# Half of the output projection's first part is queued on TensorE behind the state-space stage's last product

## The chip, the cores and the metric

The kernel runs on one core of one Trainium2 chip. The metric is the device time of one execution in microseconds (us); the time before is the median of three runs. The profile is one further execution of the same program. The engines are named as in its views: PE is TensorE's matmuls and PEld its weight loads, DVE is VectorE, ACT is ScalarE, POOL is GpSimd, SP is SyncE, which issues most DMAs.

## The reference, cut to what matters

A backbone of two layers over 512 latent tokens and 256 context tokens, 1024 channels wide. In each layer one input projection feeds three parallel branches; their outputs are joined to 2048 channels and go through one output projection.

```python
for l in range(2):
    u = rmsnorm(h, norm_w[l]) * (1 + scale) + shift          # scale, shift, gate: from mod_w[l]
    parts = split(u @ w_in[l])
    ssd = ssd_branch(...)    # 1024 channels: chunked scan over 6 chunks of 128 tokens, both directions;
                             # y * silu(z), then an RMS norm over each of two halves (g = 0, 1)
    gla = gla_branch(...)    # 512 channels
    s5  = s5_branch(...)     # 512 channels, ends in a gated product with s5_glu_w
    h = h + gate * (concat(ssd, gla, s5) @ w_out[l])         # w_out[l]: 2048 x 1024
return rmsnorm(h_lat, final_norm_w)
```

In the second layer only the latent tokens are needed at the end.

## The kernel before, in words

The kernel is written against a framework that takes the instructions in program order, each with a rank by that order, and plans the order of every engine's queue by a simulation of its own; on the chip each queue is then worked off in that order. Nothing in the source fixes the order around the change: what is ready in the planner's simulation and ranks highest goes first, and an instruction of lower rank fills an engine that would be free.

Activations lie with channels on the partitions: 128 channels by 768 tokens, of which 256 are context. Every large product is made of three passes in a split float format (`PASSES`): weights and activations are each split into a high and a low half, `wsplit` (L408 the load `wr`, ACT the copy `wh`, DVE at L411 the difference `wl`) and `split` (ACT, DVE L416). The tiles `wr`, `wh`, `wl` and the accumulators `pl` have two buffers each, the residual tiles `cv` three, the tiles `cs` three, and the operand tiles `hl` eight.

The end of a layer, in program order:

- The state-space stage (`ssd_parts`): six steps i, each for two head groups g. `decay` builds a 128x1024 matrix with eight ACT and eight DVE pieces each (L903 to L917), `within` multiplies it into the chunk (L934), `between` adds what comes from the neighbouring chunk (L923, L925, L929) and updates the running state (L946 to L957). POOL issues the loads that these steps need.
- The gate blocks of z and the gated product of the s5 branch (L1046, L1048, DVE L1057, L1059) and the splitting of the two other branches' outputs into eight `hl` tiles.
- `ssd_norm(g)`: loads z (L968, into `cs`), multiplies, squares, sums over the partitions with a product on PE (L975), takes the root on ACT, scales (L983) and splits into the tiles bA and bB.
- `spilled_part`, the first part of the output projection: for each of eight output tiles m, `out_part` makes 24 products into `pl` (L1082, 512 latent tokens) and in layer 0 another 24 into `pc` (L1084, 256 context tokens), from the eight `hl` tiles. DVE adds gate times product to the old residual (L1095 and L1096 in layer 0, L1091 in layer 1), and the sum is stored to `hpD` (L1104).
- In layer 0 only: `mod_cols(1, ...)` twice, for scale and shift of layer 1: eight loads of 512 KB each into `hl` tiles (L1112) and 64 small products (L203) for each. They need `hl` buffers that the first part has let go.
- The second part: `out_part(m, 0, yss, ...)` for m = 0 to 7 over the normed state-space output, again L1082 and L1084, with the sum from `hpD` added (L1121 is its load). In layer 0 the same again for the gate of layer 1 follows (`mod_tiles(1, 16, 8)`, L230 and L203), then layer 1.

Of the kernel before, what the change touches and what calls it, by code (L numbers as in the profile page):

```python
# [2 lines left out]

# [37 lines left out]
def hybrid_backbone_kernel(  # L41
# [16 lines left out]
    V, S, G, PE = nc.vector, nc.scalar, nc.gpsimd, nc.tensor  # L58
# [10 lines left out]
    def T(tag, shape, bufs, dt=F32):  # L69
        uid[0] += 1  # L70
        return sb.tile(shape, dt, tag=tag, bufs=bufs, name=f"{tag}_{uid[0]}")
# [26 lines left out]
    def ps(n=512, p=128):  # L98
        uid[0] += 1
        return psp.tile([128, 512], F32, tag="ps", bufs=3, name=f"ps_{uid[0]}")[:p, :n]  # L100

    def pa(n=512, p=128):
        uid[0] += 1
        return psp.tile([128, 512], F32, tag="pa", bufs=2, name=f"pa_{uid[0]}")[:p, :n]
# [15 lines left out]
    def act(out, in_, f, **kw):  # L120
        return S.activation(out, in_, f, **kw)  # L121
# [344 lines left out]
    def layer(l, u):  # L466
# [5 lines left out]
        def proj(blocks, m=128, ctx_too=True, src=None, early=False):  # L472

            w = wsplit(src if src is not None else wblk[l, blocks], 8 * m)
            p_l, p_c = pl(), pc() if ctx_too else None
            seq = [(k, wi, ui) for k in range(8) for wi, ui in PASSES]
            if early:
                seq.sort(key=lambda a: a[2])
            for n, (k, wi, ui) in enumerate(seq):
                st, sp = n == 0, n == 23  # L480
                lhs = w[wi][:, k * m : (k + 1) * m]
                PE.matmul(p_l[:m], lhs, u[k][:, ui, LC:NT], start=st, stop=sp)  # L482
                if ctx_too:
                    PE.matmul(p_c[:m], lhs, u[k][:, ui, 0:LC], start=st, stop=sp)  # L484
            return p_c, p_l
# [19 lines left out]
        p_c, p_l = proj(None, m=64, src=wdl[l], early=last)  # L505
# [70 lines left out]
        for i in range(4):  # L576
            p_c, p_l = proj(BU + i, early=last and i == 0)
# [91 lines left out]
        for b4 in range(8):  # L669
            py = pa(4 * ncx)  # L670
# [209 lines left out]
        def ssd_parts(g, i):  # L880

            wk = wgs[g]
            cf, cbk = STEPS[i]
            c = cf
            xtok, bT, cT = xts[g], bcs[g][:, 0, :], bcs[g][:, 1, :]
            rf, rbw, ex, q2 = (wk[:, 1024 * j : 1024 * j + 1024].rearrange("p (h t) -> p h t", h=8) for j in range(4))
            hs = [wk[:, 4096 + 512 * d : 4608 + 512 * d] for d in range(2)]
            xw, bt = wk[:, 5632:6144], bts[g]
            y_at = lambda c: xy[:, 4 * g : 4 * g + 4, 128 * c : 128 * c + 128]

            reads = [i > 0 and not (last and cc < 2) for cc in (cf, cbk)]
            inner = not (last and c < 2)

            def load():

                gdma(wk[:, 0:2048].rearrange("p (d x) -> p d x", d=2),
                     bass.AP(tensor=acsD[l].tensor, offset=acsD[l][c, 0, 8 * g].offset,
                             ap=[[0, 128], [2048, 2], [1, 1024]]))

            def decay():  # L900
                pcb = pa(384)
                cb, cbl, cbu = (pcb[:, 128 * j : 128 * j + 128] for j in range(3))
                PE.matmul(cb, bT[:, 128 * c : 128 * c + 128], cT[:, 128 * c : 128 * c + 128], start=True, stop=True)  # L903
                V.tensor_tensor(cbl, cb, LE, MUL)
                V.tensor_tensor(cbu, cb, GE, MUL)
                for h in range(8):
                    ih = 16 * c + 8 * g + h
                    jd = 32 * c + 8 * g + h
                    act(q2[:, h, :], cbl, AF.Copy, scale=dtt[:, jd : jd + 1])
                    V.scalar_tensor_tensor(q2[:, h, :], cbu, dtt[:, jd + 16 : jd + 17], q2[:, h, :], MUL, ADD)  # L910
                for h in range(8):
                    ih = 16 * c + 8 * g + h
                    act(ex[:, h, :], rf[:, h, :], AF.Identity, bias=naf[:, ih : ih + 1])
                    V.scalar_tensor_tensor(ex[:, h, :], rbw[:, h, :], rb[:, ih : ih + 1], ex[:, h, :], SUB, MIN)
                exf, q2f = ex.rearrange("p h t -> p (h t)"), q2.rearrange("p h t -> p (h t)")
                act(exf, exf, AF.Exp)
                V.tensor_tensor(exf, exf, q2f, MUL)  # L917

            def incoming(d, cc, ep):

                po = ps()
                for t in range(4):
                    PE.matmul(po[:, 128 * t : 128 * t + 128], hs[d][:, 128 * t : 128 * t + 128],  # L923
                              cT[:, 128 * cc : 128 * cc + 128], start=True, stop=True)
                V.tensor_tensor(po, po, ep, MUL)  # L925
                return po

            def add(cc, p):
                V.tensor_tensor(y_at(cc), y_at(cc), p.rearrange("p (t x) -> p t x", t=4), ADD)  # L929

            def within():
                py = ps()
                for h in range(8):
                    PE.matmul(py[64 * (h % 2) : 64 * (h % 2) + 64, 128 * (h // 2) : 128 * (h // 2) + 128],  # L934
                              xtok(c)[:, 64 * h : 64 * h + 64], ex[:, h // 2 + 4 * (h % 2), :], start=True, stop=True)
                add(c, py)

            def between():
                for d, cc in ((0, cf), (1, cbk)):
                    if reads[d]:  # L940
                        add(cc, incoming(d, cc, eps[eput[0] % 3]))
                        ep_load(eput[0] + 3)
                        eput[0] += 1
                    if i < 5:
                        wv = wf[:, d, 16 * cc + 8 * g : 16 * cc + 8 * g + 8]
                        V.tensor_tensor(heads(xw), heads(xtok(cc)), per_head(wv), MUL)  # L946
                        pt = pa(128)
                        PE.transpose(pt, bT[:, 128 * cc : 128 * cc + 128], ident)
                        act(bt, pt, AF.Copy)
                        pst = ps()  # L950
                        PE.matmul(pst, bt, xw, start=True, stop=True)  # L951
                        if i == 0:
                            act(hs[d], pst, AF.Copy)
                        else:
                            jd = 32 * cc + 16 * d + 8 * g
                            V.tensor_tensor(heads(hs[d]), heads(hs[d]), per_head(dec[:, jd : jd + 8]), MUL)
                            V.tensor_tensor(hs[d], hs[d], pst, ADD)  # L957

            none = lambda: None
            return (decay, within, between, load) if inner else (none, none, between, none)  # L960
# [32 lines left out]
        wgs = [big("bA"), big("bB")]  # L993
        bts = [T("bt", [128, 128], 2) for _ in range(2)]

        eps = [wgs[0][:, 5120:5632], wgs[1][:, 5120:5632], T("s5p", [128, 576], 1)[:, 0:512]]
        eput = [0]
        euse = [(g, d, cc) for i in range(1, 6) for g in range(2) for d, cc in enumerate(STEPS[i]) if not (last and cc < 2)]

        def ep_load(n):  # L1000
            if n < len(euse):
                g, d, cc = euse[n]
                gdma(eps[n % 3], bass.AP(tensor=expD[l].tensor, offset=expD[l][cc, d, 8 * g].offset,
                                         ap=[[512, 2], [0, 64], [1, 512]]))
# [32 lines left out]
        for m in range(4):  # L1037
            wv = wsplit(wglu[l, m])
            pair = []
            for half in range(2):  # L1040
                p_l, p_c = pl(), None if last else pc()
# [31 lines left out]
        def out_part(m, k0, rhs, order):  # L1073
            nk = len(rhs)
            w = wsplit(wout[l, m, k0 // 8, :, 128 * (k0 % 8) : 128 * (k0 % 8) + 128 * nk], 128 * nk)
            p_l, p_c = pl(), None if last else pc()
            n = 0
            for kk in order:
                for wi, ui in PASSES:
                    lhs = w[wi][:, kk * 128 : kk * 128 + 128]  # L1080
                    st, sp = n == 0, n == 3 * nk - 1
                    PE.matmul(p_l, lhs, rhs[kk][:, ui, LC - t0 : NT - t0], start=st, stop=sp)  # L1082
                    if not last:
                        PE.matmul(p_c, lhs, rhs[kk][:, ui, 0:LC], start=st, stop=sp)  # L1084
                    n += 1
            return p_c, p_l
# [10 lines left out]

        def spilled_part(src, k0, rhs, order):
            for m in range(8):
                p_c, p_l = out_part(m, k0, rhs, order)  # L1100
                ho = cv(NT)
                dma(ho[:, t0:NT], src[128 * m : 128 * m + 128])
                residual(ho, ho, m, p_c, p_l)
                dma(hpD[l][128 * m : 128 * m + 128, t0:NT], ho[:, t0:NT])  # L1104
# [13 lines left out]
        for m in range(8):  # L1118
            p_c, p_l = out_part(m, 0, yss, range(len(yss)))
# [155 lines left out]
```

## Time and profile before

| | us |
|---|---|
| median of 3 runs | 1627.29 (1621.0 to 1630.99) |
| the profiled execution | 1629.74 |
| its span, first to last instruction | 1628.0 |
| PE busy | 1385.0 |
| DVE busy | 1216.1 |
| ACT busy | 651.1 |

The profiled execution is 1.7 us longer than its span and 2.4 us above the median of the runs. The mean granted clock of TensorE was 0.911 of its full 2.4 GHz.

### The profile page before, as it was taken

To read this page: it belongs to the slowest core of one execution; us is meant where nothing else is said; L and a number is where in the kernel's file an instruction comes from. 1 tells how busy PE (TensorE), PEld (TensorE's weight loads), DVE (VectorE), ACT (ScalarE), POOL (GpSimd) and SP (SyncE) were. 2 spreads that over 40 slices of the span, in tenths; PEclk is the share of its full clock that TensorE was granted. 3 is DMA by queue.
4 is the path that set the end of the run, shared out by engine and by line. 5 is a ranking of instruction groups with operands and counts; after the bars stand their busy time and mean duration, and the time that the engine had idled before them with its cause. 6 is when DMAs were issued, how large, how long until landed. Compare 5 with 4: busy or idle time off the path is not lost.

```text
span 1628.0 us, 23300 instructions
## 1 busy us (share of the span) xinstructions
PE 1385.0 (85%) x8536; PEld 1123.9 (69%) x8536; DVE 1216.1 (75%) x2487; ACT 651.1 (40%) x1159; POOL 110.4 (7%) x248
## 2 busy tenths in 40 slices
PE   3879885899499889998994898998989999979766
PEld 2657774778496766776872585887779887756545
DVE  8767757999478894499896636369966897798964
ACT  4212224222623622565442524334363446554452
POOL 0000001310000000001010000041000000010100
PEclk8889978999589989999997899999989999999978
DMA  8566567332155535446668432642336443446522
GB/s 324 139 140 194 155 162 191 101 117 82 34 167 162 188 99 157 129 153 179 219 214 274 154 123 90 181 152 91 121 114 186 124 142 124 137 136 198 169 71 97
DMA packets 154658, 243.85 MB, mean 150 GB/s; under 512 B 48688, under 2 KB 89648, under 8 KB 154544
## 3 DMA queue, kind: packets, MB, share of 16 engines
q1 hardware_dynamic: 130096, 211.82, 42.8%
q0 software_dynamic: 24448, 30.54, 6.6%
q8 instruction: 67, 1.10, 0.3%
q14 instruction: 47, 0.39, 0.1%
HBM read 192.81 MB, written 49.38 MB: 149 GB/s over the span
## 4 chain that ended last, share of the span: by engine, by line
PE 45%; DVE 25%; DMA 16%; ACT 7%; issue 6%; SPq 1%; DVEq 0%; ACTq 0%; POOLq 0%
PE pl L482 13%; PE pl L1082 9%; PE pc L484 4%; DMA gD<-cs 4%; DMA bc<-lpD 3%; PE pc L1084 3%; ACT bA L121 2%; DMA cs<-zD 2%; DVE wl L411 2%; PE ps L951 2%; PE pl L1046 1%; PE pl L704 1%; PE ps L923 1%; PE pa L392 1%; ACT bB L121 1%
## 5 line engine op out<-in xcount | busy, mean ns | idle before, releaser
L482 PE MATMUL pl<-hl,wh 128*128 128x512 f32 (+1 forms) x1184 | 405.4, 410 | 18.8 <-DVE ev L501 14.5
L482 PEld LDWEIGHTS pl<-hl,wh 128*128 128x128 f32 (+1 forms) x1184 | 223.8, 193 | 75.0 <-DVE ev L501 15.1
L482 PE MATMUL pl<-hl,wl 128*128 128x512 f32 (+1 forms) x592 | 241.6, 409 | 18.1 <-DVE wl L411 18.1
L121 ACT ACTIVATE wh<-wr 128x1024 fp32r<-128x1024 f32 (+1 forms) x122 | 127.9, 1051 | 286.4 <-PE pc L484 95.7
L411 DVE TENSOR_TENSOR wl<-wr,wh 128x1024 fp32r<-128x1024 f32 (+1 forms) x122 | 147.8, 1213 | 66.1 <-ACT wh L121 52.8
L484 PE MATMUL pc<-hl,wh 128*128 128x256 f32 (+1 forms) x864 | 189.9, 293 | 5.8 <-ACT hl L121 4.7
L484 PEld LDWEIGHTS pc<-hl,wh 128*128 128x128 f32 (+1 forms) x864 | 145.2, 193 | 16.4 <-issue 5.7
L482 PEld LDWEIGHTS pl<-hl,wl 128*128 128x128 f32 (+1 forms) x592 | 114.4, 193 | 49.5 <-DVE wl L411 22.6
L484 PE MATMUL pc<-hl,wl 128*128 128x256 f32 (+1 forms) x432 | 126.4, 293 | 0.0
L1082 PE MATMUL pl<-hl,wh 128*128 128x512 f32 x256 | 87.9, 416 | 6.9 <-ACT hl L121 2.4
L484 PEld LDWEIGHTS pc<-hl,wl 128*128 128x128 f32 (+1 forms) x432 | 83.1, 192 | 5.2 <-issue 3.6
L704 PE MATMUL pl<-wh,hl 128*128 128x256 f32 x384 | 78.6, 303 | 2.0 <-ACT ev L121 2.0
L121 ACT ACTIVATE ev<-pl 128x512 f32<-128x512 f32 (+1 forms) x98 | 51.9, 532 | 57.0 <-PE pl L704 22.9
L852 DVE SCALAR_TENSOR_TENSOR xy<-ev,par_sb,xy 128x256 f32<-128x256 f32 (+1 forms) x128 | 73.2, 610 | 0.5
L704 PEld LDWEIGHTS pl<-wh,hl 128*128 128x128 f32 x384 | 65.0, 207 | 7.4 <-ACT ev L121 3.0
L392 PE MATMUL pa<-cs 64*32 64x128 f32 x512 | 42.3, 297 | 27.4 <-DVE cs L398 14.8
L1082 PEld LDWEIGHTS pl<-hl,wh 128*128 128x128 f32 x256 | 48.0, 193 | 20.8 <-ACT hl L121 3.2
L704 PE MATMUL pl<-wl,hl 128*128 128x256 f32 x192 | 57.5, 302 | 0.0
L392 PEld LDWEIGHTS pa<-cs 64*32 64x32 f32 x512 | 21.9, 112 | 44.6 <-DVE cs L398 15.5
L1082 PE MATMUL pl<-hl,wl 128*128 128x512 f32 x128 | 51.9, 407 | 0.3 <-DVE wl L411 0.3
L1046 PE MATMUL pl<-hl,wh 128*128 128x512 f32 x128 | 43.2, 409 | 10.4 <-ACT cv L121 6.8
L121 ACT ACTIVATE cs<-pa 64x128 f32<-64x128 f32 (+1 forms) x66 | 15.6, 263 | 87.9 <-PE pa L392 82.8
(468 smaller groups left out, 3032.3 us busy)
## 6 DMA issues: line engine op xcount, KB each, us to landing
wr<-in_wblk SPq DMA_DIRECT2D x80, 512.0 KB
wr<-in_wout SPq DMA_DIRECT2D x32, 512.0 KB
hl<-in_mod_w SPq DMA_DIRECT2D x20, 512.0 KB
bA<-acsD POOLq DMA_DIRECT2D x10, 1024.0 KB, 7.4
bB<-acsD POOLq DMA_DIRECT2D x10, 1024.0 KB, 10.1
clD<-cs SPq DMA_DIRECT2D x64, 128.0 KB
cs<-clD SPq DMA_DIRECT2D x32, 256.0 KB
cs<-in_mod_w SPq DMA_DIRECT2D x16, 512.0 KB
```

What stands on the lines that cost most here:

```text
L121: return S.activation(out, in_, f, **kw)
L392: PE.matmul(pk[d][32 * gg : 32 * gg + 32], b0[64 * d : 64 * d + 64, a, :], w54[64 * d : 64 * d + 64, a, gg, d : 8 + d, :].rearrange("p k h ...
L411: V.tensor_tensor(wl, wr, wh.bitcast(F32), SUB)
L482: PE.matmul(p_l[:m], lhs, u[k][:, ui, LC:NT], start=st, stop=sp)
L484: PE.matmul(p_c[:m], lhs, u[k][:, ui, 0:LC], start=st, stop=sp)
L704: PE.matmul(p, u[k][:, ui, 128 * c : 128 * c + 128], ws[k // 4][wi][:, 256 * (k % 4) : 256 * (k % 4) + 256], start=n == 0, stop=n == 23)
L852: V.scalar_tensor_tensor(ac, raw[:, o + k : o + k + n], pcol("cw", w0 + k), ac, MUL, ADD)
L923: PE.matmul(po[:, 128 * t : 128 * t + 128], hs[d][:, 128 * t : 128 * t + 128], cT[:, 128 * cc : 128 * cc + 128], start=True, stop=True)
L951: PE.matmul(pst, bt, xw, start=True, stop=True)
L1046: PE.matmul(p_l, lhs, yg5[k][:, ui, LC:NT], start=n == 0, stop=n == 11)
L1082: PE.matmul(p_l, lhs, rhs[kk][:, ui, LC - t0 : NT - t0], start=st, stop=sp)
L1084: PE.matmul(p_c, lhs, rhs[kk][:, ui, 0:LC], start=st, stop=sp)
```

## The change

Every product that `out_part` traces for m = 4 to 7 of the first part, in both layers, gets an ordering edge to the last product of the stage that was traced before it: the last of the eight products of `within` for g = 1 in step 5. The edge is on TensorE's queue alone and adds no wait on a semaphore: the planner may not put these products ahead of that one. The loads, splits, residual adds and stores of these four tiles get no edge.

```diff
             def within():
                 py = ps()
                 for h in range(8):
-                    PE.matmul(py[64 * (h % 2) : 64 * (h % 2) + 64, 128 * (h // 2) : 128 * (h // 2) + 128],
+                    inner_last[0] = PE.matmul(py[64 * (h % 2) : 64 * (h % 2) + 64, 128 * (h // 2) : 128 * (h // 2) + 128],
                               xtok(c)[:, 64 * h : 64 * h + 64], ex[:, h // 2 + 4 * (h % 2), :], start=True, stop=True)
                 add(c, py)
...
+        inner_last = [None]
...
         def spilled_part(src, k0, rhs, order):
             for m in range(8):
-                p_c, p_l = out_part(m, k0, rhs, order)
+
+                with tc.issue_after(inner_last[0].ins) if m >= 4 else nullcontext():
+                    p_c, p_l = out_part(m, k0, rhs, order)
                 ho = cv(NT)
                 dma(ho[:, t0:NT], src[128 * m : 128 * m + 128])
                 residual(ho, ho, m, p_c, p_l)
```

`tc.issue_after(ins)` gives every instruction that the block traces on the engine of `ins` an edge behind `ins`.

## Rows read from the trace of the kernel before

**Rows 1.** Timeline of SP, DMA issues: start, us, line, what is loaded or stored.

```profile
803.93 0.38 SPq L1104 DMA_DIRECT2D hpD<-cv  x1
...
847.63 5.40 SPq L1112 DMA_DIRECT2D hl<-in_mod_w  x8
853.85 0.33 SPq L1104 DMA_DIRECT2D hpD<-cv  x1
...
1494.85 0.37 SPq L1104 DMA_DIRECT2D hpD<-cv  x1
...
1525.42 0.32 SPq L1104 DMA_DIRECT2D hpD<-cv  x1
```

**Rows 2.** Timeline of PE, both layers: start, us, line, count, idle before and releaser.

```profile
879.28 1.09 PE L934 MATMUL ps<-bB,cs 128*64 128x128 f32 x16
894.24 2.90 PE L975 MATMUL ps<-ev,ones 128*128 128x256 f32 x4 [13.86 <-DVE ev L433]
...
910.22 3.66 PE L203 MATMUL pl<-hl,sc 128*32 128x256 f32 x64
...
1500.70 1.09 PE L934 MATMUL ps<-bB,cs 128*64 128x128 f32 x16
...
1548.89 1.97 PE L934 MATMUL ps<-bB,cs 128*64 128x128 f32 x16 [4.67 <-DVE bB L917]
```

**Rows 3.** The chain that ended last, layer 0 (first three) and layer 1: start, us, what.

```profile
849.50 10.99 DMA hl<-in_mod_w
...
926.14 5.50 PE pl L1082 x24
931.64 2.87 PE pc L1084 x24
...
1581.16 29.61 PE pl L1082 x130
```

**Rows 4.** Windows: stretch, busy us and count of PE, PEld, DVE, ACT, POOL; clock; DMA.

```profile
804.00:879.30 75.30, 64.38 (x447) 49.17 (x445) 61.69 (x134) 29.84 (x81) 7.86 (x10) 0.91 0.80 242
879.30:984.50 105.20, 83.76 (x528) 66.50 (x527) 54.07 (x69) 36.29 (x42) 0.00 (x0) 0.89 0.45 152
1495.00:1548.90 53.90, 41.16 (x241) 32.45 (x240) 50.25 (x107) 25.10 (x62) 5.51 (x7) 0.92 0.56 176
1548.90:1610.80 61.90, 50.43 (x203) 37.60 (x204) 34.44 (x48) 27.23 (x36) 0.00 (x0) 0.85 0.23 73
...
804.00:850.30 46.30, 46.30 (x303) 38.70 (x302) 41.74 (x91) 19.56 (x53) 6.29 (x8) 1.00 0.65 199
...
879.30:919.00 39.70, 18.26 (x153) 8.92 (x153) 28.03 (x35) 20.93 (x25) 0.00 (x0) 0.70 0.59 199
...
1495.00:1524.60 29.60, 29.60 (x161) 23.25 (x161) 27.50 (x59) 14.21 (x36) 3.95 (x5) 1.00 0.69 223
...
1530.60:1548.90 18.30, 7.31 (x50) 6.62 (x50) 16.87 (x38) 7.11 (x17) 0.78 (x1) 0.76 0.35 105
1548.90:1573.70 24.80, 14.06 (x46) 8.41 (x47) 16.66 (x27) 15.62 (x21) 0.00 (x0) 0.62 0.15 43
```

**Rows 5.** Windows of one line each: L411 twice, L1095, L1096, L1091 (DVE busy).

```profile
804.00:879.30 75.30, 4.87 (x4) 0.91 0.80 242
...
1495.00:1548.90 53.90, 4.88 (x4) 0.92 0.56 176
...
804.00:879.30 75.30, 1.91 (x4) 0.91 0.80 242
...
804.00:879.30 75.30, 2.98 (x4) 0.91 0.80 242
...
1495.00:1548.90 53.90, 2.98 (x4) 0.92 0.56 176
```

**Rows 6.** Waits, 804 to 879.3: the longest of PE; us, times, longest us.

```profile
PE pl L203 <- DMA hl<-in_mod_w: 8.0, 6, 2.6
```

More of the change, by code (lines that the diff above doesn't have):

```diff
@@ L1 @@
 import math
-from contextlib import ExitStack
+from contextlib import ExitStack, nullcontext
 import concourse.bass as bass
```

## Prediction

> **What bounds the kernel now.** I read the granted clock and the page first: TensorE is the busiest engine, so the question is where it has no work in the stages that the change touches. Then the timelines of SP and PE, to place the edge. The stores of the residual sums tell when each output tile of the first part was done: in layer 0 tile 3's store is issued at 803.9 and tile 7's at 853.9, in layer 1 at 1494.9 and 1525.4 [rows 1]. The product that the change names starts at 879.3 and at 1548.9 [rows 2]. So tiles 4 to 7 ran from about 804 to 850 and from 1495 to 1525, wholly ahead of it, in both layers: the edge binds, and it moves all four tiles.
>
> Third, the windows [rows 4]. While tiles 4 to 7 run, PE is busy in all 46.3 us of layer 0's stretch and all 29.6 us of layer 1's, at a granted clock of 1.00, and the chain of waits lies on PE there. But DVE is busy 41.7 of the 46.3 us (0.90) and 27.5 of the 29.6 us (0.93): with PE relieved, DVE is the next bound, after a gain of only 7 to 10 per cent. Behind the named product it is the other way round: in 879.3 to 984.5, to the end of layer 0's second part, PE works 83.8 of 105.2 us, and in 1548.9 to 1610.8, the same in layer 1, 50.4 of 61.9. The norm of the state-space output runs there, and its sum product waits 13.9 us for DVE [rows 2].
>
> The sum needs four terms for each layer: what the state-space stage gains by losing the four tiles, what PE gets to do behind the named product, how much of that falls into idle time, and new waits.
>
> **What is removed ahead of the named product.** From PE 4 x (5.5 + 2.9) = 33.4 us in layer 0 and 4 x 5.5 = 21.9 us in layer 1, by the second part's tiles of the same shape: 24 products in 5.50 and 2.87 us [rows 3], and 130 in 29.61, which is 5.47 for 24. What counts is how much earlier DVE lets the named product come. DVE works 61.7 us in 804 to 879.3. Four residual adds (1.9 + 3.0 us) and four weight splits (4.9 us, those of tiles 6 and 7 and of the second part's first two, since only two buffers of each exist) go with the tiles [rows 5]: 51.9 us are left. At the share at which DVE works in the packed stretch of layer 0 (0.90) and in layer 1's stretch without any tile, 1530.6 to 1548.9 (16.9 of 18.3 us, 0.92) [rows 4], that takes 56 to 58 us in place of 75.3. The bounds: 51.9 us if DVE never waits (23.4 earlier), and 63 us at the mean share of the stretch now, 61.7 of 75.3 (12 earlier). I take **18 us earlier in layer 0**. Part of it is the 11 us at 849.5 in which the chain waits for loads of in_mod_w [rows 3]: products of `mod_cols` stand in PE's queue ahead of state-space products, and PE itself waits 8.0 us for them [rows 6]. They need buffers that tile 7 frees, so they move behind the named product too.
>
> Layer 1, the same way: 50.3 us of DVE in 53.9, less 3.0 and 4.9 [rows 4, 5], leave 42.4; at 0.90 to 0.92 that is 46 to 47 us. Bounds 42.4 (11.5 earlier) and, at the present 0.93 with two more microseconds for handovers at a lower clock, 48 or, if handovers cost more, 50 (4 earlier). I take **7.5 us earlier**.
>
> **What is added behind it.** Layer 0: 33.4 us of tiles and the first 64 products of `mod_cols`, 3.7 us at full clock [rows 2], 37.1 in all. PE's idle time there is 105.2 - 83.8 = 21.4 us. Work that is there now at the lower clock would run faster on a PE kept busy: 18.3 us at 0.70 before 919 [rows 4] would shrink by some 5 us. Against it the first products behind the named one start cold: I put 2 us, an estimate by L934's 1.97 for 1.09 us [rows 2]. 37.1 - 21.4 - 5 + 2 = **12.7 us later**, counted from the named product. Layer 1: 21.9 us added, 61.9 - 50.4 = 11.5 us idle, 14.1 us at 0.62 before 1573.7 [rows 4] that shrink by some 5, 2 for the cold start: **7.4 us later**.
>
> So the gaps behind the named product do not hold what is moved into them. The change pays only as far as the state-space stage shortens, and that is DVE's.
>
> **New waits.** No semaphore is added, but the order of queues changes. On PE, `mod_cols` and the second part stand behind the four tiles. The 16 loads of 512 KB for `mod_cols` now start when tile 7 ends and land while the second part runs; the eight of the first half were issued over 5.4 us [rows 1] and cost PE 8.0 us of waiting when the planner had put their products among others [rows 6]. The planner's idea of their landing has not changed, so I expect about as much again, now among the second part's products and wholly on the path. The bounds are 3 us (the second part's products between them cover most) and 14 (the second half waits as well, which today hides in the norm's gap). On SP these loads come behind the z loads, no longer among them; quicker z loads make the norm earlier, which is worth nothing if PE is the later one, and it is. On DVE four residual adds and four splits, 9.8 us in layer 0, now stand between the norm's operations; a residual add waits for its tile, with the norm queued behind it. PE has the other tiles to do meanwhile, so only a late second group of the norm shows: 0 to 5 us, inside the values above. POOL's queue holds nothing of this. I take **7 us in layer 0** and **2 us in layer 1** (0 to 5), which has no `mod_cols`.
>
> **The sum.** Layer 0: -18 + 12.7 + 7 = +1.7. Layer 1: -7.5 + 7.4 + 2 = +1.9. Together +3.6 us on the profiled 1629.7, 1633.3; the median of the runs lies 2.4 us lower, so **1631 us**. One per cent, about what a measurement here can tell from no change, is 16 us: the forecast is no change that can be told.
>
> **The rivals.** First, slower: TensorE is cold in the state-space stage, which then does not shorten. With the tiles in it the clock is 1.00 (1495 to 1524.6), without them 0.76 (1530.6 to 1548.9), the stretch behind has 0.62 [rows 4], and 16 products of L934 take 1.97 us where they took 1.09 [rows 2]. The stage's own products are 64.4 - 33.4 - 3.7 = 27 us in layer 0 and 41.2 - 21.9 = 19 in layer 1, mostly at full clock now; at half clock they take up to as much again, each between two DVE steps of its group. If 9 us of that come onto the path in each layer, the gain of 25.5 us falls to 7.5, and 12.7 + 7 + 7.4 + 2 - 7.5 = +21.6, 1649; if the whole gain goes, +29, 1656. It decides from the point where the named product comes less than 12.7 us earlier in layer 0 and 7.4 in layer 1. The Trainium skill, "TensorE: Matmul & The Clock Gate", Part 1, has the rule that speaks against this change: an array that idles is throttled to half rate and has to earn its full clock back. By that rule alone the sum would be this rival's; the trace agrees on the two levels, and it has the two head groups to cover for each other, as in 1530.6 to 1548.9, where DVE is busy for 0.92 at the lower clock. Chance 0.24.
>
> Second, faster: DVE runs without a gap (23.4 and 11.5 us earlier) and the new waits do not appear: -23.4 + 12.7 - 11.5 + 7.4 = -14.8, 1612. For more than that the planner's new order would have to shorten something else. For it speaks that the 11 us behind in_mod_w fall out of the stage in any case; against it, that DVE never did better than 0.93 in any of these stretches. Chance 0.17.
>
> Third, the edge does nothing, because these products ran late anyway: excluded by the stores above, unless the edge gets lost. 1627. Chance 0.03.
>
> **How the numbers follow.** The forecast, 1618 to 1643, has 0.56. The range takes in most of the faster rival and the slower one to the half of its price: 1610 to 1650. Faster by over 1% needs nearly all of the second rival's value, or some more, 0.13; slower by over 1% is the first rival, 0.24; the rest, 0.63, lies between.
>
> **What would show it.** The four tiles behind the last L934 in both layers; that product at about 861 and, counted from tile 3's store in layer 1, some 47 us behind it; DVE over 0.88 busy from tile 3 to there; PE without a gap over 3 us from there to the second part's end, except in front of L203 in layer 0. Wrong would be: the named product hardly earlier (first rival), second parts that end earlier by more than 5 us in each layer (second rival), or a difference that arises elsewhere, in the projections ahead of these stages, by another plan.

## The result, and the profile after

The changed kernel takes 1641.4 us (median of 8 runs, 1636.4 to 1650.1) beside 1629.1 us (8 runs, 1619.1 to 1634.6) for the kernel before: ratio **1.0093**, 95% interval 1.0066 to 1.012. That is some 15 us by the ratio and 12.2 by the medians. The forecast was 1631 us, with 1610 to 1650 as its range. The profiled execution has a span of 1636.4 us and took 1638.1 us. In this kernel the lines of the output projection stand one to three further down: L1083 and L1085 are the products, L1107 is the store of `hpD`, L1115 the load for `mod_cols`.

The edge does what it says in both layers. The timeline of SP (start, us, line, transfer) answers to [rows 1]:

```profile
796.08 0.38 SPq L1107 DMA_DIRECT2D hpD<-cv  x1
...
864.23 0.32 SPq L1107 DMA_DIRECT2D hpD<-cv  x1
...
888.56 5.45 SPq L1115 DMA_DIRECT2D hl<-in_mod_w  x8
...
900.06 0.33 SPq L1107 DMA_DIRECT2D hpD<-cv  x1
...
1496.47 0.32 SPq L1107 DMA_DIRECT2D hpD<-cv  x1
...
1561.43 0.32 SPq L1107 DMA_DIRECT2D hpD<-cv  x1
```

Tile 3's sums are stored at 796.1 and 1496.5, tile 4's at 864.2 and 1561.4; the loads for `mod_cols` begin 41 us later than before, as tile 7 frees its `hl` buffers. The timeline of PE (with the idle time before a group and what ended it) answers to [rows 2]:

```profile
852.64 1.09 PE L934 MATMUL ps<-bB,cs 128*64 128x128 f32 x16 [1.07 <-DVE bB L917]
...
894.74 0.92 PE L203 MATMUL pl<-hl,sc 128*32 128x256 f32 x8 [2.04 <-DMA hl<-in_mod_w]
...
915.30 0.99 PE L203 MATMUL pl<-hl,sc 128*32 128x256 f32 x8 [1.91 <-DMA hl<-in_mod_w]
...
1527.21 1.09 PE L934 MATMUL ps<-bA,m 128*64 128x128 f32 x16
...
1546.88 1.98 PE L934 MATMUL ps<-bB,cs 128*64 128x128 f32 x16 [14.04 <-DVE bB L917]
```

In layer 0 the named product comes at 852.64, 56.6 us behind tile 3's store instead of 75.4. In layer 1 it comes at 1546.88, only 2 us before its old place, and PE stands idle 14 us ahead of it, with four tiles ready that the edge keeps back. The windows answer to [rows 4]:

```profile
796.10:852.70 56.60, 31.29 (x190) 22.09 (x191) 53.66 (x124) 27.28 (x77) 7.87 (x10) 0.79 0.40 117
...
1546.90:1621.60 74.70, 72.46 (x309) 57.96 (x310) 40.06 (x53) 30.46 (x39) 0.00 (x0) 0.95 0.33 111
853.70:890.90 37.20, 37.20 (x211) 31.23 (x210) 30.73 (x40) 21.15 (x23) 0.00 (x0) 1.00 0.63 211
890.90:923.00 32.10, 25.48 (x237) 12.61 (x236) 8.33 (x13) 3.94 (x7) 0.00 (x0) 0.78 0.96 374
923.00:985.60 62.60, 62.60 (x341) 54.56 (x340) 21.54 (x28) 14.43 (x18) 0.00 (x0) 0.98 0.38 127
1495.00:1546.90 51.90, 24.41 (x153) 16.81 (x151) 45.48 (x102) 21.46 (x59) 5.52 (x7) 0.77 0.35 109
1527.00:1546.90 19.90, 3.36 (x37) 2.86 (x35) 14.87 (x32) 6.02 (x13) 0.79 (x1) 0.74 0.25 69
```

Read the third, fourth and fifth row together. Behind layer 0's named product the tiles run dense, then come 32 us in which DVE has 8 us of work, PE is busy for 25.5 at a granted clock of 0.78, and the DMA engines are 0.96 busy at 374 GB/s, and then the second part, dense again. The chain that ended last has three pieces in that stretch (start, us, what), and they are no engine's:

```profile
892.28 8.99 DMA hl<-in_mod_w
901.29 9.92 DMA cs<-in_mod_w
911.28 10.37 DMA cs<-in_mod_w
```

The last row of the windows is layer 1's end of the stage: DVE is busy for 0.75 of it and PE for 0.17.

The time of one execution spreads by some 15 us, more than either layer's effect, so the experiments are compared by layer. The table gives for each profiled execution three times from the timeline of PE: from the start of the layer's first L934 to that of the last one (the named product), from there to the end of the second part's last product, and the sum. For the kernel before these are 691.73, 879.28 and 984.55 in layer 0. "Ratio" is that of the timed runs to the kernel before.

| kernel | layer 0 | layer 1 | ratio (95%) |
|---|---|---|---|
| before | 187.6 + 105.3 = 292.8 | 121.2 + 64.3 = 185.5 | 1 |
| changed | 166.7 + 132.9 = 299.6 | 118.5 + 74.7 = 193.2 | 1.0093 (1.0066 to 1.012) |
| e1, edge in layer 0 only | 166.8 + 132.8 = 299.5 | 120.7 + 64.5 = 185.2 | 1.0035 (1.0012 to 1.0058) |
| e2, edge in layer 1 only | 187.4 + 104.2 = 291.6 | 116.9 + 74.8 = 191.7 | 1.0027 (1.0006 to 1.0048) |
| e3, edge at g = 0, step 5 | 170.2 + 130.5 = 300.7 | 120.4 + 70.6 = 191.0 | 1.01 (1.0074 to 1.0126) |
| e4, edge at g = 1, step 4 | 171.1 + 116.9 = 288.0 | 122.1 + 68.6 = 190.7 | 1.0047 (1.0023 to 1.0071) |
| e5, changed, no mod_cols | 167.0 + 109.2 = 276.2 | 117.4 + 73.0 = 190.4 | 0.9954 (0.9932 to 0.9976) |
| e6, before, no mod_cols | 178.7 + 95.9 = 274.6 | 120.5 + 67.7 = 188.2 | 0.9896 (0.987 to 0.9923) |
| e7, changed, mod_cols late | 166.7 + 121.4 = 288.2 | 115.5 + 72.6 = 188.0 | 0.9998 (0.997 to 1.0026) |
| e8, before, mod_cols late | 185.9 + 107.5 = 293.4 | 120.9 + 64.3 = 185.2 | 1.0008 (0.9977 to 1.004) |
| e9, norm(0) behind the decay | 167.0 + 133.5 = 300.5 | 113.6 + 77.3 = 190.9 | 1.0065 (1.0032 to 1.0097) |
| e10, decay first | 165.7 + 133.4 = 299.1 | 108.2 + 79.5 = 187.7 | 1.0044 (1.0016 to 1.0072) |
| e11, step 4 and mod_cols late, layer 0 | 171.2 + 117.8 = 289.1 | 121.2 + 63.9 = 185.2 | 0.9983 (0.9952 to 1.0013) |
| e12, parts together | 167.2 + 121.8 = 289.0 | 118.5 + 68.6 = 187.1 | 1.0004 (0.9981 to 1.0027) |

With the unedited edge in layer 0 (changed, e1, e9, e10) that layer takes 299.7 us on average, without it (before, e2) 292.2: **+7.5**. Layer 1 takes 190.8 with it (changed, e2, e5, e7) and 185.8 without (before, e1, e6, e8, e11): **+5.0**. The sum, 12.5 us, lies within the measured interval of 11 to 20. Layer 0 repeats within 1.4 us in these groups. Layer 1 repeats less well: 188.0 to 193.2 with the edge and 185.2 to 188.2 without, so its +5.0 is less firm.

### The profile page after: what moved, and what is told of

Its sections match the earlier page's. It is cut to its first block, busy times and chain, and to the rows that moved or that the text cites. A ratio compares the mean times of both kernels' runs of the same rounds, so it can differ in the third digit from the quotient of the medians.

```text
span 1636.4 us, 23309 instructions
## 1 busy us (share of the span) xinstructions
PE 1383.6 (85%) x8536; PEld 1122.2 (69%) x8536; DVE 1214.3 (74%) x2487; ACT 651.3 (40%) x1159; POOL 110.4 (7%) x248
## 4 chain that ended last, share of the span: by engine, by line
PE 24%; DVE 10%; issue 8%; DMA 5%; ACT 3%; POOL 1%; SPq 0%; DVEq 0%; ACTq 0%; POOLq 0%
PE pl L482 7%; PE pl L1083 7%; PE pc L1085 2%; PE pc L484 1%; DMA cs<-in_mod_w 1%; PE pl L704 1%; ACT bB L121 1%; ACT bA L121 1%; DVE wl L411 1%; DVE xy L852 1%; PE ps L951 1%; DVE bc L852 1%; DMA hl<-in_mod_w 1%; DMA bB<-acsD 1%; DMA bB<-expD 1%
## 5 line engine op out<-in xcount | busy, mean ns | idle before, releaser
L411 DVE TENSOR_TENSOR wl<-wr,wh 128x1024 fp32r<-128x1024 f32 (+1 forms) x122 | 148.0, 1214 | 64.0 <-ACT wh L121 51.2
L482 PEld LDWEIGHTS pl<-hl,wl 128*128 128x128 f32 (+1 forms) x592 | 113.6, 192 | 49.3 <-DVE wl L411 23.2
L1083 PE MATMUL pl<-hl,wh 128*128 128x512 f32 x256 | 86.3, 409 | 8.2 <-ACT hl L121 3.7
L121 ACT ACTIVATE ev<-pl 128x512 f32<-128x512 f32 (+1 forms) x98 | 51.9, 532 | 87.2 <-PE pl L704 31.1
L704 PE MATMUL pl<-wh,hl 128*128 128x256 f32 x384 | 75.1, 294 | 2.4 <-ACT ev L121 2.4
L1083 PEld LDWEIGHTS pl<-hl,wh 128*128 128x128 f32 x256 | 47.9, 191 | 23.3 <-ACT hl L121 4.8
L1083 PE MATMUL pl<-hl,wl 128*128 128x512 f32 x128 | 51.2, 402 | 0.6 <-DVE wl L411 0.6
L121 ACT ACTIVATE bB<-bB 128x1024 f32<-128x1024 f32 (+3 forms) x22 | 34.4, 1562 | 38.9 <-DVE bB L757 24.9
```

What stands on the lines that cost most here:

```text
L411: V.tensor_tensor(wl, wr, wh.bitcast(F32), SUB)
L704: PE.matmul(p, u[k][:, ui, 128 * c : 128 * c + 128], ws[k // 4][wi][:, 256 * (k % 4) : 256 * (k % 4) + 256], start=n == 0, stop=n == 23)
```

## The experiments

The theory after the first look: in layer 0 the time goes to the loads for `mod_cols`, which now can't start before tile 7 is done; in layer 1 DVE's planned order holds the named product, and with it the tiles. The rivals were TensorE's amount of work, its lower clock, or an effect in one layer alone.

### Which layer: e1 and e2

```
-                with tc.issue_after(inner_last[0].ins) if m >= 4 else nullcontext():
+                with tc.issue_after(inner_last[0].ins) if m >= 4 and not last else nullcontext():   # e1
+                with tc.issue_after(inner_last[0].ins) if m >= 4 and last else nullcontext():       # e2
```

> The edge stands in layer 0 alone; layer 1 queues its four tiles as before. Theory: the change costs about 7 us in layer 0 (the state-space stage is 19 us shorter, but TensorE gets 28 us more from the named product to the end of the second part) and 8 us in layer 1, so this kernel takes 1634 to 1638 us, ratio 1.003 to 1.006. Rival 1: layer 0 carries all of the 15 us, because what layer 1 lost is only the clock of one execution: ratio 1.008 to 1.011. Rival 2: layer 1 carries all of it: ratio 0.998 to 1.001.

> The edge stands in layer 1 alone. Theory: the 8 us of layer 1, 1635 to 1639 us, ratio 1.003 to 1.006; the named product (last L934) comes 2 to 4 us earlier than in the kernel before, counted from the first L934 of the layer, and TensorE stands idle about 14 us ahead of it for DVE's bB. Rival 1 (layer 0 carries all): ratio 0.999 to 1.001. Rival 2 (layer 1 carries all): 1.008 to 1.011.

Measured 1.0035 and 1.0027. Both layers carry a part, layer 0 about 6 us and layer 1 about 4, and the two rivals that put all in one layer fall: neither ratio reaches 1.008, and the interval of e1 lies above 1.001.

### An earlier anchor: e3 and e4

```
-                    inner_last[0] = PE.matmul(py[...
+                    inner_last[0 if (g, i) == (0, 5) else 1] = PE.matmul(py[...   # e3; e4: (1, 4)
```

> The edge starts at the last product of step 5 of the first group of heads instead of the second group's; in layer 1 that product ends at 1527 us and TensorE then stands idle for 14 of the 20 us up to the named product. Theory (layer 1's loss is this idle time, in which four ready tiles are kept back): most of two tiles or more, 8 to 13 us, move into it without delaying the named product by more than 3, so layer 1 comes out at -5 to +1 against the kernel before; layer 0, where the two products lie 5 us apart, stays at +5 to +8. In all 1629 to 1637 us, ratio 1.000 to 1.005. Rival (TensorE's amount of work decides: whatever goes ahead of the named product pushes it back by as much): ratio 1.008 to 1.011, as with the change.

> The edge starts at the last product of step 4 of the second group, which ends at 1524 us in layer 1 and about 12 us ahead of the named product in layer 0. Theory: layer 1 as with the edge at the first group's step 5, or 1 to 3 us better, since the tiles can start 3 us sooner; layer 0 gains 0 to 5 us, because some tiles end sooner and the buffers that the modulation's loads wait for come free sooner. In all 1625 to 1635 us, ratio 0.997 to 1.004. Rival (whatever goes ahead of the named product pushes it back by as much): ratio 1.006 to 1.011.

For e3 my theory missed, in layer 1 and in all; the ratio, 1.01, is the one that the rival gave. But the rival's mechanism is not what the trace shows. The four tiles did move into the idle time, and the named product came only 3 us later than the average of the kernels with the edge (120.4 for 117.1), but the layer still ended at 191.0. The timeline of PE in e3 shows what is late next:

```profile
1550.33 1.09 PE L934 MATMUL ps<-bB,cs 128*64 128x128 f32 x16
...
1561.20 1.22 PE L1083 MATMUL pl<-bA,wh 128*128 128x512 f32 x2 [7.33 <-ACT bA L121]
...
1570.67 1.02 PE L975 MATMUL ps<-ev,ones 128*128 128x512 f32 x2
...
1577.86 1.22 PE L1083 MATMUL pl<-bB,wh 128*128 128x512 f32 x2 [5.24 <-ACT bB L121]
```

The norm's second sum (L975) stands in PE's queue behind second-part products that wait for bA, and DVE then waits 5.6 us for it (L976), so the second group's bB is there only 27.5 us behind the named product, where the kernel before has it after 22.9 (its product of bB at 1571.77). Empty slots of PE are not the only limit; the norm's chain behind the named product is another.

e4 came out the way the theory had it in layer 0, and by more: the last tile ends at 877.1 instead of 891.3, and the layer takes 288.0, 11.6 us less than in the changed kernel, where 0 to 5 had been put. That was the first sign that the end of tile 7, through what it frees, sets the end of layer 0. Layer 1 gained nothing. The total (1.0047, 0.997 to 1.004 expected) is above the time that these two layers would give (+1 us); one profiled execution does not tell that difference of some 6 us from spread.

### Layer 0: mod_cols left out (e5, e6) or later (e7, e8)

```
 if not last:
-    for b0 in (8, 0): ... mod_cols(1, b0, 8, rows, ...)
+    V.memset(modp[:, 1, 0:16, :], 0.0)                      # e5 (changed kernel), e6 (kernel before)

 second part, loop over m:
+    if m == 3 and not last:                                 # e7 (changed), e8 (before); gone from its old place
+        for b0 in (8, 0): ... mod_cols(1, b0, 8, rows, ...)
```

> The changed kernel without the two mod_cols of layer 0 that make layer 1's scale and shift (they are set to zero, so 16 loads of 512 KB and 128 products are left out). Theory (layer 0's loss behind the named product is the wait for these loads, which can start only when the last of the four tiles frees its buffers): the stretch from 891 to 923 us, in which TensorE waits for hl<-in_mod_w, goes, the second part starts within 5 us of the last tile, and layer 0 from its first L934 to the end of the second part falls from 299.6 to 268 to 275 us; in all 1610 to 1618 us. Rival (the loss is the amount of TensorE's work, and the norm and the residual sums on DVE would fill that stretch anyway): 288 us or more there, and 1630 us or more in all.

> The same left out of the kernel before. Theory: here most of the loads lie beside the state-space stage, so less is gained: layer 0 from its first L934 to the end of the second part falls from 292 to 272 to 284 us, 1607 to 1619 us in all. Between the two kernels without mod_cols the difference in layer 0 is then -8 to +3 us, against +7 with it. Rival: the difference in layer 0 stays at +5 to +9 us, and in all this kernel is 13 to 17 us faster than the changed one without mod_cols.

> The changed kernel with all its work, and mod_cols written behind tile 3 of layer 0's second part instead of ahead of that part. Theory: the loads (8.4 MB, about 22 us at the 374 GB/s of the stretch 891 to 923) land beside the first four tiles of the second part, which take 33 us, and only the products' own 7 to 10 us stay on the path: layer 0 from its first L934 to the end of the second part at 276 to 285 us, 1617 to 1627 us in all, below the changed kernel by 15 to 24. Rival (the loads take the queues and the bandwidth from the weights and the z rows wherever they lie): 295 us or more there, 1635 us or more.

> The kernel before with mod_cols written behind tile 3 of layer 0's second part. Theory: the 11 us behind in_mod_w in the state-space stage and the waits behind the named product go, the products' 7 to 10 us stay: layer 0 at 276 to 288 us from its first L934 to the end of the second part, 1611 to 1623 us in all; the changed kernel with the same edit then differs from it by -6 to +3 us in layer 0 and by 4 to 8 us in layer 1, where nothing is edited. Rival: no shorter than 290 us.

Without `mod_cols`, layer 0 is 276.2 us with the edge and 274.6 without: of the difference of 6.8 between the two profiled kernels 1.6 is left. The medians of the timed runs agree: e5 and e6 differ by 7.5 us (1615.7 and 1608.2), the kernels with `mod_cols` by 12.2. In e5 the second part follows the tiles at once (windows):

```profile
853.30:891.90 38.60, 38.60 (x227) 32.39 (x228) 32.14 (x42) 21.42 (x23) 0.00 (x0) 1.00 0.60 208
891.90:962.50 70.60, 70.60 (x404) 59.26 (x407) 28.83 (x38) 16.68 (x20) 0.00 (x0) 1.00 0.41 142
```

So `mod_cols` costs the changed kernel 23.4 us (299.6 - 276.2), all of it behind the named product, and the kernel before 18.2 (292.8 - 274.6), of which 8.9 lie in the state-space stage. The rival, by which DVE would fill that stretch anyway, falls. e5 gained a little less than I expected (276.2, not 268 to 275). Products for the gate (`mod_tiles`) stay in its second part, 404 in the window for 384 of its own; that they are the reason is not shown.

With all its work and `mod_cols` written behind tile 3 of the second part, the changed kernel gains 11.4 us in layer 0, to 288.2, some 3 us less than expected. The second part with 128 small products in it is dense (e7's window from its start; it is 12.4 us longer than e5's above, and PE is busy for all but 1 us of it):

```profile
884.00:967.00 83.00, 81.95 (x564) 64.27 (x565) 29.64 (x40) 17.65 (x22) 0.28 (x1) 1.00 0.62 234
```

In the kernel before the same edit gained nothing (e8, 293.4), against the theory. The likely reason is in its trace: all the products moved, but only the second eight loads did (to 931 us). The first eight still start when tile 7 frees its buffers, in the middle of the stage (timeline of SP),

```profile
836.15 5.70 SPq L1126 DMA_DIRECT2D hl<-in_mod_w  x8
```

and there DVE waits for a load of the stage itself (the list of waits, 839 to 869: us, times, longest):

```profile
DVE ps L925 <- DMA s5p<-expD: 7.1, 1, 7.1
```

In e6, without these loads, DVE has no wait for a load there. Between e7 and e8 the edge makes no difference that the runs tell (0.9998 and 1.0008): it is 5.2 us shorter in layer 0, as expected, and 2.8 us longer in layer 1, where 4 to 8 had been put.

### Layer 1: DVE's order (e9, e10)

The timeline of DVE in the changed kernel, from which the theory came:

```profile
1532.63 0.35 DVE L910 SCALAR_TENSOR_TENSOR bB<-pa,dts,bB 128x128 f32<-128x128 f32 x1
1532.88 1.29 DVE L970 TENSOR_TENSOR xy<-xy,cs 128x512 f32<-128x512 f32 x2
1537.70 0.70 DVE L925 TENSOR_TENSOR ps<-ps,bA 128x512 f32<-128x512 f32 x1 [3.52 <-DMA bA<-expD]
...
1538.90 0.34 DVE L910 SCALAR_TENSOR_TENSOR bB<-pa,dts,bB 128x128 f32<-128x128 f32 x1
...
1539.76 0.68 DVE L433 TENSOR_TENSOR ev<-ev,cs 128x512 f32<-128x512 f32 x1
1540.36 0.68 DVE L970 TENSOR_TENSOR xy<-xy,cs 128x512 f32<-128x512 f32 x1
1540.96 0.34 DVE L910 SCALAR_TENSOR_TENSOR bB<-pa,dts,bB 128x128 f32<-128x128 f32 x1
...
1545.12 0.34 DVE L910 SCALAR_TENSOR_TENSOR bB<-pa,dts,bB 128x128 f32<-128x128 f32 x1
1545.50 1.23 DVE L917 TENSOR_TENSOR bB<-bB 128x1024 f32<-128x1024 f32 x1
```

L917 lets the named product go. The pieces of its decay matrix (L910) stand one by one between operations of the first group's norm (L970, L433), which lead to nothing urgent, and an add (L925) that waits 3.5 us for its load.

```
-                V.tensor_tensor(exf, exf, q2f, MUL)                                   # L917
+                decay_last[0] = V.tensor_tensor(exf, exf, q2f, MUL)
-        yss = ssd_norm(0) + ssd_norm(1)
+        with tc.issue_after(decay_last[0].ins) if last else nullcontext():            # e9, e10
+            yss = ssd_norm(0)
+        yss += ssd_norm(1)
-                parts[g][i][2]()
+                with tc.issue_after(decay_last[0].ins) if last and (g, i) == (1, 5) else nullcontext():   # e10 only
+                    parts[g][i][2]()
```

> The changed kernel, with the operations of ssd_norm(0) on DVE queued in layer 1 behind the last decay operation (L917) of the second group's step 5. Theory (DVE's order, not its amount of work or TensorE's clock, holds the named product in layer 1): from 1532.9 to 1545.1 us the last four L910 and L917 stand between seven L970 and L433 of the norm and behind a wait of 3.5 us for DMA bA<-expD; without the norm's operations the named product comes 2 to 5 us earlier, 111.5 to 116.5 us behind the layer's first L934 in place of 117 to 118.5, and the layer ends 1 to 5 us earlier, the wait for expD staying. Rival (TensorE at the lower clock and the hand-overs between ACT and DVE hold it): no earlier than 116.5 us, and the layer ends no earlier.

> As the run with the norm queued later, and in layer 1 the DVE operations of the second group's last between (two L925 that wait for expD, two L929) stand behind that L917 too. Theory: the decay runs on from 1529 us in eight hand-overs of some 0.7 us, so the named product comes 7 to 11 us earlier than in the changed kernel, 107 to 111.5 us behind the layer's first L934, TensorE stands idle less than 6 us ahead of it in place of 14, and from the first L934 to the end of the second part layer 1 takes 180 to 186 us (190.8 on average over the four kernels with the edge there, 186 without). The whole kernel then takes 1632 to 1637 us, the loss of layer 0 alone. Rival (clock and hand-overs): 115 us or more for the named product, 188 us or more for the layer.

The named product came 3.4 us earlier with the norm behind the decay (113.6 for 117.1 on average) and 8.9 us earlier with the adds behind it too (108.2), as the theory had it and against clock and hand-overs. e10's timelines of DVE and of PE:

```profile
1527.83 0.35 DVE L910 SCALAR_TENSOR_TENSOR bB<-pa,dts,bB 128x128 f32<-128x128 f32 x1 [0.43 <-ACT bB L121]
1528.62 0.35 DVE L910 SCALAR_TENSOR_TENSOR bB<-pa,dts,bB 128x128 f32<-128x128 f32 x1 [0.43 <-ACT bB L121]
...
1531.36 1.23 DVE L917 TENSOR_TENSOR bB<-bB 128x1024 f32<-128x1024 f32 x1
```

```profile
1532.73 1.97 PE L934 MATMUL ps<-bB,cs 128*64 128x128 f32 x16 [4.88 <-DVE bB L917]
...
1565.47 0.50 PE L1084 MATMUL pl<-bB,wh 128*128 128x512 f32 x1 [1.08 <-ACT bB L121]
```

But the layer's end followed only in part. With e9 it did not move (190.9), a miss; with e10 it is 187.7, outside what I had put (180 to 186), 3.1 us below the average with the edge and 1.9 above that without. Behind the named product the rest grew from 73.8 to 77.3 and 79.5 us: the norm's operations were only put off, and the second part now has waits in it. Behind the named product PE is busy for 72.5 of 74.7 us in the changed kernel and for 74.7 of 79.5 in e10, so its own work is most of what is left there. In all e10 measured 1.0044, near the 1.0035 of the edge in layer 0 alone.

### The parts put together: e11 and e12

```
 e11: the edge in layer 0 only, anchor (g, i) == (1, 4) as in e4, mod_cols behind tile 3 as in e7
 e12: the edge in layer 0 only, named anchor, mod_cols behind tile 3; in layer 1 no edge, DVE's order of e10
```

> Layer 1 as in the kernel before; in layer 0 the edge starts at step 4's last product of the second group, and mod_cols stands behind tile 3 of the second part. Theory: with the earlier edge the last tile ends 191 us behind the first L934 in place of 205, and with mod_cols behind tile 3 the second part starts at once and takes 83 us: layer 0 to the end of the second part at 274 to 281 us (292 before), in all 1610 to 1619 us, faster than the kernel before by 0.6 to 1.1 per cent. Rival (the norm's chain of about 22 us behind the named product, or loads that collide, takes the place): 284 us or more, no difference in all.

> In layer 0 the edge with mod_cols behind tile 3 of the second part; in layer 1 no edge, but DVE's order of the decay-first run. Layer 0 goes from its first L934 to the end of the second part in 286 to 290 us (288.2 with the same edits before, 292 in the kernel before). For layer 1, theory: the decay order is a gain of its own, also where the four tiles lie ahead of the named product; that product comes 3 to 5 us earlier (116 to 118 us behind the first L934 in place of 121) and, since the norm's chain behind it ends the layer, the layer is 2 to 5 us shorter (180 to 184 us); in all 1615 to 1622 us, 0.994 to 0.998 of the kernel before. Rival: the norm's operations, now behind the decay, come as much later as the named product comes earlier; the layer stays at 184 to 188 us, in all 1619 to 1626 us, ratio 0.996 to 1.0.

e11 went the rival's way: 289.1 in layer 0, 0.9983 in all. Tiles and `mod_cols` are out of the way, and now the norm is late (timeline of PE):

```profile
857.98 1.09 PE L934 MATMUL ps<-bB,cs 128*64 128x128 f32 x16
...
883.23 0.79 PE L1083 MATMUL pl<-bA,wh 128*128 128x512 f32 x1 [5.38 <-ACT bA L121]
...
898.90 0.50 PE L1083 MATMUL pl<-bB,wh 128*128 128x512 f32 x1 [0.98 <-ACT bB L121]
...
901.68 0.50 PE L1083 MATMUL pl<-bB,wh 128*128 128x512 f32 x1 [1.92 <-DVE bB L416]
```

e12 too: the named product of layer 1 came 2.4 us earlier than without the edge (118.5 for 120.9), the layer no shorter (187.1). No version that does all the work beats the kernel before by more than the measurement tells; e11 is the lowest of them, with 1 in its interval.

## Why the time came out 10 us above the prediction

**What bounds the stage, right in layer 0.** The term was -18; counted from tile 3's store it is -18.8. DVE has 53.7 us of work in 56.6, where 51.9 in 56 to 58 was put. By e6 and e5 some 9 us of the shorter stage are `mod_cols` leaving it (187.6 to 178.7) and 11.7 are the tiles (178.7 to 167.0).

**The first rival, TensorE cold in the stage, falls for layer 0.** The granted clock did go to 0.79 in the stage, where it was 0.91 [rows 4], so by the clock the rival and the Trainium skill's page "TensorE: Matmul & The Clock Gate", Part 1, had it right. It cost little there: DVE was busy for 0.95 of the stage, which leaves 2.9 us for all waits together. In layer 1 the clock was 0.77 in the stage, and the product came only 3.9 us earlier, which by the prediction's own sign (less than 7.4) speaks for the rival. e10 decides against it: its edit touches DVE's queue alone, and the named product came 8.9 us earlier than with the edge alone.

**The tiles behind the named product, about right.** Layer 1: 73.8 us for 64.9 on average, +8.9, where 7.4 and 2 were put. Layer 0 without `mod_cols`: 109.2 for 95.9 (e5, e6), +13.3. The prediction's 12.7 contains 3.7 us of `mod_cols`; without them its working gives 9.0 (33.4 - 21.4 - 5 + 2). PE's idle time there is smaller in e6 than the 21.4 us of the kernel before, 96.0 - 80.7 = 15.3 us (windows of e6):

```profile
860.00:882.00 22.00, 7.96 (x34) 3.53 (x33) 17.25 (x23) 11.07 (x14) 0.00 (x0) 0.64 0.56 179
882.00:956.00 74.00, 72.72 (x443) 60.65 (x444) 35.15 (x45) 24.85 (x29) 0.07 (x1) 0.99 0.42 140
```

With 15.3 in place of 21.4 the same working gives 15.1, near the measured 13.3.

**The new waits of layer 0: the term that was mis-sized.** I put 7 us, with 3 to 14 as bounds, "about as much again" as the 8.0 us of waiting now [rows 6]. PE's waits for these loads did stay that small (list of waits of the changed kernel, 850 to 990: us, times, longest):

```profile
PE pl L203 <- DMA hl<-in_mod_w: 6.3, 9, 2.0
```

But the delay is more than the idle time. Between the waits PE worked at a granted clock of 0.78, and the second part stood behind. With the same work queued so that the loads are covered (e7), the time behind the named product falls from 132.9 to 121.4: **11.5 us**, where 7 was put. As a whole `mod_cols` costs 23.7 us behind the named product in the changed kernel (132.9 - 109.2), and 9.4 in the kernel before (105.3 - 95.9): 14.3 more, where 3.7 of products and 7 of waits were put. What I left out is the amount: 16 loads of 512 KB are 8.4 MB, and four of the eight loads for the gate (`cs<-in_mod_w`, 512 KB each), which the prediction doesn't name, were issued into the same stretch, at 894.8 to 911.3. At 374 GB/s 8.4 MB alone are 22 us. In the kernel before all 16 were issued beside the stage, from 847.6 to 876.1, and the gate's eight in the norm's gap, from 900.7 to 918.9. Now the 16 start at tile 7's end with no work of equal length left to cover them but the second part, of which all but 48 products stand behind theirs in PE's queue. That the stretch is the DMA engines' is read from the chain and the windows of the changed kernel. e5 shows that it goes without `mod_cols`, loads and products together; e7 shows that it goes with both kept, when they are queued where the loads are covered.

**Layer 1's shortening: the other one.** I put -7.5 (bounds -4 to -11.5) on DVE's amount of work at a busy share of 0.90 to 0.92. It is -3.9 on average and -2.7 in the profiled execution; DVE's busy share was 0.88 over the stage and 0.75 in its last 20 us. The step that failed is that DVE would do the stage's work first and densely: its queue holds the norm's operations and waits for loads between the last pieces of the decay. e9 and e10 show that order, and not amount, held the product. That little of this gain reaches the layer's end is seen in both, too; what bounds the end there (the norm's chain, or PE's own work, of which twelve tiles at 5.47 us are 66 us) is argued from the rows of e3, e10 and e11, not taken apart further.

**The sum.** Layer 0 +7.5 instead of +1.7, layer 1 +5.0 instead of +1.9: 8.9 us of the 10 between 1631 and 1641. Some 2 us more are the starting point: the forecast was built on 1627.3 us for the kernel before, which took 1629.1 in the later runs. In layer 0 a part of the miss is hidden by luck: counted from the first L934 the stage is 20.9 us shorter, and 2.1 of them lie ahead of tile 3's store, where the prediction has no term. The range held the result. The change stayed just under the one per cent that the forecast took as the mark of what can be told; but the interval lies clear of 1, so the runs do tell it from no change.

## What to carry to other kernels

Moving work behind a late point moves what that work frees, too: before holding back a consumer, list the loads that wait for its buffers, add up their bytes, and ask which work is left to cover them. Where one engine's queue is the bound, read the order of its last few microseconds before multiplying its work by a busy share. And an idle slot of TensorE that is filled pays only if no other chain (here the norm's) ends at the same place; e3, e9, e11 and e12 each made something earlier that didn't end last.

## What the runs showed of the hardware

Loads beside the stage went with a slower landing of the stage's own small ones. The 256 KB loads of `expD` that POOL issues (issue to landing, us, in the last column) took in the kernel before, from 850 to 880 us beside `mod_cols`' loads,

```profile
bA<-expD POOLq DMA_DIRECT2D x1, 256.0 KB, 18.3
```

and in e6, without those loads,

```profile
bA<-expD POOLq DMA_DIRECT2D x1, 256.0 KB, 8.6
```

In the changed kernel it is 7.5 us, so a part of layer 0's earlier product may be this. It was not separated from the other effects of moving `mod_cols` out of the stage.

The stretch 890.9 to 923.0 moved 374 GB/s. The Trainium skill, "DMA: Bandwidth & Descriptors", Specifications, has about 358 GB/s as the memory limit of one core, half of its stack's 716. This kernel runs on a single core, and the measured stretch lies above that figure; the measurement decides here.

Two executions differed by 11 us where no instruction does. From layer 0's end to the first L934 of layer 1 e7 takes 446.5 us and e12 457.2, with every engine's queue in the same order there. The two ran on different chips, and the clock differs (windows of e12, then of e7):

```profile
1169.60:1269.60 100.00, 91.54 (x558) 81.99 (x557) 60.00 (x118) 45.00 (x55) 5.52 (x26) 0.80 0.46 132
```

```profile
1166.70:1266.70 100.00, 92.15 (x629) 82.83 (x628) 65.58 (x131) 51.80 (x66) 6.43 (x31) 0.88 0.51 150
```

Why the one execution had the lower clock there is open. It is the reason for reading such small effects by layer.
